# Four modulation vectors of a diffusion layer: three summed by the vector engine during the value and latent projections, one left on the tensor engine

## The chip, the cores and the metric

The kernel runs on one core of a Trainium2 chip. The metric is the device time of one execution in microseconds (us), lower is better; for each kernel the median of several runs is compared.

## What is computed

The reference is one layer of a diffusion backbone over 512 latent tokens with 256 context tokens, model width 1024, all in float32. What matters here is where the modulation vectors come from and where they are used:

```python
sh1, sc1, g1, sh2, sc2, g2 = adaln(c, w_mod, b_mod)        # silu(c) @ w_mod + b_mod, split in six rows of 1024
hx = modulate(rmsnorm(x, norm_attn_g), sh1, sc1)           # h * (1 + scale) + shift
proj = hx @ w_in                                           # queries, latents, keys, values
o_mla = mla_latent_attention(...)                          # latent attention, 8 heads
o_na = neighbourhood_attention(...)                        # 8 x 16 window, 8 heads
mixed = concat(o_mla, o_na) @ w_out
x = x + g1 * mixed
hx2 = modulate(rmsnorm(x, norm_ffn_g), sh2, sc2)
x = x + g2 * hierarchical_moe(hx2, ...)                    # 16 experts, 2 chosen per token
return rmsnorm(x, final_norm_g)
```

`sh1` and `sc1` are needed at once. The four later rows, `g1`, `sh2`, `sc2` and `g2`, are a product of one vector of 1024 numbers with a matrix of 1024 x 4096 (16.8 MB, called `w_mod_b` in the kernel). `g1` is first used when the output projection begins, `sh2` and `sc2` before the experts, `g2` in the experts.

## The kernel before, in words

A float32 product is made of three matmuls (`mm3`, L56 to L59): each operand is split into a rounded high part (ScalarE, a cast) and the rest, the low part (VectorE, a subtraction), and the products high x high, high x low and low x high are summed. `load_split` (L183) loads a weight into one of three buffers `raw` by SyncE's queue and splits it into `wh` and `wl`, two buffers each. ScalarE (ACT), VectorE (DVE), TensorE (PE), GpSimd (POOL) and SyncE (SP, which issues DMAs) run in order, each through its own list; a scheduler of the framework orders these lists from the order of the code and what depends on what.

The stages, with the time at which they run in the profile: normalisation, first modulations and values (`v_part`, to 66 us; the normalised and transposed rows `xnt` are last read by `mod_h`, L274); the key-value latents (L351 to L363: 3 weight batches, 6 row tiles in PSUM banks 0 to 5, to 85 us); the query latents (L364 to L375: 4 weight batches, to 102 us); norms, transposes and the first projections of neighbourhood attention (to 124 us); neighbourhood attention proper (L720 to L793, 32 blocks: 4 pairs p of heads, 2 heads u, 4 query tiles i, to 241 us); latent attention; output projection and routing; 16 experts (from 427 us).

The four later modulations are computed by `mod_rest` (L510), called for every second of the 32 blocks (L746). Each of its 16 calls loads two tiles of `w_mod_b` (128 x 1024, 512 KB each) into `raw` and issues four matmuls of 512 columns on TensorE, with the vector `silu(c)` as a stationary operand of 32 columns (`sstat`, column 0 is the vector, most are zero), at four column positions of the array, so that the four give four parts of the row. 8 calls make the sums of two vectors; after the last of them the bias is added (L525) and the result stored in DRAM as `mod_d` (L526), from where the later stages load it.

The change and the prediction's steps touch `mod_rest`, the pools around `xnt` (L190 to L192), the latents' loops (L351 to L375), what follows them on VectorE (L385 to L416) and the block loop. TensorE's matmuls in float32 appear twice in the trace for each instruction.

Of the kernel before, what the change touches and what calls it, by code (L numbers as in the profile page):

```python
# [8 lines left out]
F32 = mybir.dt.float32  # L9
# [4 lines left out]
OP = mybir.AluOpType  # L14
# [3 lines left out]
P = 128  # L18
D = 1024
KT = 8  # L20
# [18 lines left out]
def hybrid_kernel(tc, nc, x_k, x_q, ctx, cvec, w_mod_a, w_mod_b, b_mod_c, b_mod_r, g_ffn_row,  # L39
                  w_v, w_kv, w_ql, w_qk, g_q, g_kv, w_uq, w_ukv, rel, w_out_a, w_out_b, w_r, b_r,  # L40
                  w_gate, w_up, w_down, g_fin_row, cpk0, cpk, out):
    sy, ac, ve, pe, gp = nc.sync, nc.scalar, nc.vector, nc.tensor, nc.gpsimd

    def pool(name, bufs=1, side="left", space=None):
        kw = dict(name=name, bufs=bufs, reuse_waits="tile")
        if space is None:
            return tc.alloc_tile_pool(side=side, **kw)
        return tc.alloc_tile_pool(space=space, **kw)
# [30 lines left out]
    def copy(dst, src, of=2):  # L79
        turn[0] += 1  # L80
        if turn[0] % of == 1:
            ve.tensor_copy(dst, src)
        else:
            ac.copy(dst, src)
# [60 lines left out]
    gp.dma_start(wr, w_r)  # L145
    gp.dma_start(brb, b_r.to_broadcast([P, 20]))


    chp = pool("chp")
    omp = pool("omp")  # L150
# [13 lines left out]
    sstat = navp.tile([P, KT, 32], F32, name="sstat")  # L164
# [5 lines left out]
    HW = CX + TC  # L170
# [7 lines left out]
    def load(src, n=1024):  # L178
        r = raw_tile()
        sy.dma_start(r[:, :n], src)  # L180
        return r

    def load_split(src, n=1024, r=None):  # L183
        r = load(src, n) if r is None else r
        h = chp.tile([P, 1024], F32R, name="wh", tag="wh", bufs=2)
        l = chp.tile([P, 1024], F32R, name="wl", tag="wl", bufs=2)
        split(h[:, :n], l[:, :n], r[:, :n])
        return h, l

    pa = pool("pa", side="right")  # L190
    xnt = pa.tile([P, KT, HW], F32, name="xnt")
    px = pool("px", side="right")  # L192
    xts = []

# [7 lines left out]
    def bank(*nums):  # L202

        n = taken[nums] = taken.get(nums, -1) + 1
        return psA.tile([P, 512], F32, name="ps", tag=f"b{nums[n % len(nums)]}", bufs=1)
# [105 lines left out]
    def v_part(k, ts):  # L311
        wv_h, wv_l = wv[k // 2]
        s = slice(k % 2 * 512, k % 2 * 512 + 512)
        for t in ts:
            mm3(av[t], hh[:, k, key_cols(t)], hl[:, k, key_cols(t)], wv_h[:, s], wv_l[:, s],
                start=(k == 0), stop=(k == KT - 1))
# [22 lines left out]
    for q in range(2, 4):  # L339
        for k in (2 * q, 2 * q + 1):  # L340
            mod_h(k, 0)
            mod_h(k, 1)
            v_part(k, range(6))
    for t in range(6):
        copy(nav[:, t, :], av[t])


    px.release()
    pl = pool("pl", side="right")
    KB = (0, 3, 6, 8)  # L350
    akv = [bank(i) for i in range(6)]  # L351
    for b in range(3):
        n = KB[b + 1] - KB[b]
        wh, wl = load_split(w_kv[:, KB[b] * 288:KB[b + 1] * 288], n * 288)
        for i in range(n):
            k = KB[b] + i
            s = slice(i * 288, (i + 1) * 288)
            for t in range(6):
                mm3(akv[t][:, 0:288], hh[:, k, key_cols(t)], hl[:, k, key_cols(t)], wh[:, s], wl[:, s],
                    start=(k == 0), stop=(k == KT - 1))  # L360
# [3 lines left out]
    aq = [bank(i) for i in range(4)]  # L364
    for b in range(4):
        wh, wl = load_split(w_ql[b], 768)
        for i in range(2):
            k = 2 * b + i
            s = slice(i * 384, (i + 1) * 384)
            for t in range(4):  # L370
                mm3(aq[t][:, 0:384], hh[:, k, q_cols(t)], hl[:, k, q_cols(t)], wh[:, s], wl[:, s],
                    start=(k == 0), stop=(k == KT - 1))
    qlt = pl.tile([P, 4, 384], F32, name="qlt")
    for t in range(4):
        copy(qlt[:, t, :], aq[t][:, 0:384])  # L375

    krk = pl.tile([P, 6, 32], F32, name="krk")

# [16 lines left out]
    for c in range(2):  # L395
        for b0, n in ((0, 4), (4, 2)):
            tr = bank4(4, 5, 6)
            for i in range(n):
# [5 lines left out]
                                    op0=OP.mult, op1=OP.subtract)  # L404
# [18 lines left out]
    sy.dma_start(qn_dram, qst)  # L423

    pl.release()
    pa.release()


# [36 lines left out]
    nw = pool("nw", side="right")  # L465
# [37 lines left out]
    ve.memset(zero, 0.0)  # L503


    mod_d = tc.dram_tile([2, 4, 512], F32, name="mod_d")
    modf = mod_d.rearrange("r a b -> r (a b)")
    mod_ps = []

    def mod_rest(n):  # L510
        r, k = divmod(n, KT)
        if k == 0:
            br = nw.tile([P, 512], F32, name="br", tag="br", bufs=1)
            ve.memset(br, 0.0)
            rows = br.rearrange("(a b) n -> a b n", b=32)[:, 0, :]
            sy.dma_start(rows, b_mod_r[r])
            mod_ps[:] = bank(7), br, rows
        ps, br, rows = mod_ps
        ws = [load(w_mod_b[r, k, :, q * 1024:(q + 1) * 1024]) for q in range(2)]
        for g in range(4):  # L520
            pe.matmul(ps[g * 32:(g + 1) * 32, :], sstat[:, k, :],
                      ws[g // 2][:, g % 2 * 512:g % 2 * 512 + 512], start=(k == 0), stop=(k == KT - 1),
                      tile_position=(0, g * 32))
        if k == KT - 1:
            ve.tensor_tensor(br, br, ps, op=OP.add)  # L525
            sy.dma_start(mod_d[r], rows)  # L526

    na_heads, na_w, na_ps = {}, {}, {}

# [190 lines left out]
    for b, (p, u, i) in enumerate(blocks):  # L720
        w = b % 8
# [21 lines left out]
        if w == 0 and p:  # L743
            norm_ = normalise_steps(na_ssum[p - 1], nw, onh[:, p - 1, :], onl[:, p - 1, :])
            next(norm_)
        if i % 2:  # L746
            mod_rest(p * 4 + u * 2 + i // 2)
        pull(NS[p][w] - (NS[p][w] > 1))
        if w == 0 and p:
            norm_.send((na_values(p - 1), bank4(4, 5)))  # L750
# [139 lines left out]
    mw = pool("mw")  # L890
# [1028 lines left out]
```

## Time and profile before

| | |
|---|---|
| median of 3 runs | 736.14 us (732.59 to 736.38) |
| the profiled execution | 733.54 us, of which the profile's span is 731.8 us |
| TensorE busy | 698.1 us (95%) |
| VectorE busy | 546.4 us (75%) |
| ScalarE busy | 447.7 us (61%) |
| DMA | 174.6 MB, mean 239 GB/s |

The page of the profile gives the busy time of each engine over the span. A busy share is an average over stages with different limits, so for a change that moves work from one stage to another the stretches are read one by one: how busy each engine is there, and what each engine waited for. "PEld" is the load of stationary operands, which overlaps the matmuls.

### The profile page before, as it was taken

The page shows a single profiled execution, that of the slowest core. Times are in us where ns is not written, and L with a number is a line of the kernel's source. Part 1 is how long each engine was busy: PE and PEld are TensorE (multiplying, and loading weights), DVE is VectorE, ACT ScalarE, POOL GpSimd, SP SyncE. Part 2 cuts the span into 40 slices and gives each one's busy share as a digit, 9 for nine tenths or more (in the row PEclk, how much of TensorE's full clock was granted, in tenths as well). Part 3 has the DMA queues.
Part 4 walks back from the last instruction along what each step waited for, and adds up shares of the span by engine and source line. Part 5 has one row for each costly group of instructions (what it writes and reads, how often), then busy time and mean ns, then how long its engine had stood idle before and what let it go on. Part 6 is the DMA issues. An engine that isn't in the chain of part 4 may idle for free. (4 is left out here: it accounts for less than half of the span.)

```text
span 731.8 us, 10466 instructions
## 1 busy us (share of the span) xinstructions
PE 698.1 (95%) x3918; PEld 516.9 (71%) x3919; DVE 546.4 (75%) x749; ACT 447.7 (61%) x698; POOL 83.7 (11%) x56
## 2 busy tenths in 40 slices
PE   4999999999999999999999679999999999999995
PEld 3678997767765887868658557777777777777773
DVE  4572457766676795656536778999999999999996
ACT  6451355654555455646644377777777777777763
POOL 1010000000000000000010122222222222221310
PEclk9999999999999999999999769999999999999998
DMA  8931238555476821121179979999999999999673
GB/s 319 409 124 60 73 95 279 194 172 190 144 236 202 288 88 43 60 76 54 59 252 364 346 244 364 362 372 370 353 360 357 358 352 350 358 354 379 239 132 116
DMA packets 39336, 174.58 MB, mean 239 GB/s; under 512 B 5711, under 2 KB 7191, under 8 KB 26992
## 3 DMA queue, kind: packets, MB, share of 16 engines
q1 hardware_dynamic: 34880, 163.72, 61.4%
q0 software_dynamic: 4112, 10.06, 6.3%
q8 instruction: 32, 0.52, 0.3%
q14 instruction: 24, 0.20, 0.1%
q10 hardware_dynamic: 288, 0.08, 0.0%
HBM read 163.00 MB, written 14.79 MB: 243 GB/s over the span
## 5 line engine op out<-in xcount | busy, mean ns | idle before, releaser
L1376 DVE TENSOR_TENSOR el<-ew,eh 128x2048 fp32r<-128x2048 f32 (+1 forms) x106 | 220.6, 2087 | 17.3 <-ACT eh L1373 13.7
L1373 ACT CAST eh<-ew 128x1024 fp32r<-128x1024 f32 x190 | 190.1, 1050 | 43.9 <-PE s L59 29.4
L57 PE MATMUL s<-eh,xh 128*96 128x512 f32 x260 | 104.7, 403 | 1.1 <-ACT xh L62 1.1
L59 PE MATMUL s<-eh,xl 128*96 128x512 f32 x260 | 103.3, 397 | 0.0
L58 PE MATMUL s<-el,xh 128*96 128x512 f32 x260 | 102.8, 395 | 0.0
L1588 POOL DMA_INDIRECT ya_d<-yo,idx x14 | 45.5, 3251 | 140.7 <-DVE yo L1592 140.7
L59 PEld LDWEIGHTS s<-eh,xl 128*96 128x96 f32 x260 | 42.3, 163 | 19.3 <-DVE xl L63 0.7
L57 PEld LDWEIGHTS s<-eh,xh 128*96 128x96 f32 x260 | 42.4, 163 | 18.3 <-ACT xh L62 1.4
L58 PEld LDWEIGHTS s<-el,xh 128*96 128x96 f32 x260 | 42.5, 164 | 17.5 <-DVE el L1376 0.2
L57 PE MATMUL y<-eh,ghh 128*96 128x512 f32 x120 | 48.2, 401 | 0.0
L59 PE MATMUL y<-eh,ghl 128*96 128x512 f32 x120 | 47.3, 394 | 0.0
L58 PE MATMUL y<-el,ghh 128*96 128x512 f32 x120 | 47.2, 393 | 0.0
L470 DVE TENSOR_REDUCE nm<-s 128x1 f32<-128x768 f32 x32 | 30.5, 954 | 19.1 <-PE s L59 18.9
L57 PE MATMUL ps<-wh,hh 128*128 128x512 f32 (+2 forms) x128 | 43.9, 345 | 0.5 <-ACT hh L275 0.3
L59 PE MATMUL ps<-wh,hl 128*128 128x512 f32 (+2 forms) x128 | 43.5, 345 | 0.2 <-DVE hl L277 0.2
L58 PE MATMUL ps<-wl,hh 128*128 128x512 f32 (+2 forms) x128 | 43.4, 341 | 0.0
L1303 POOL MEMSET xg<- 128x1024 f32 x2 | 1.9, 954 | 322.1 <-DMA g<-mod_d 322.1
L57 PE MATMUL ps<-hh,wh 128*128 128x512 f32 (+1 forms) x96 | 36.4, 379 | 0.0
L946 ACT ACTIVATE pr<-s,nm 128x768 f32<-128x768 f32 x32 | 29.1, 908 | 9.8 <-DVE nm L470 9.6
L59 PE MATMUL ps<-hh,wl 128*128 128x512 f32 (+1 forms) x96 | 34.4, 359 | 0.0
L58 PE MATMUL ps<-hl,wh 128*128 128x512 f32 (+1 forms) x96 | 34.2, 357 | 0.0
L1261 POOL DMA_INDIRECT xg<-hx_d,idx x16 | 24.2, 1510 | 65.9 <-PE t L1519 46.7
(360 smaller groups left out, 1455.8 us busy)
## 6 DMA issues: line engine op xcount, KB each, us to landing
ew<-w_gate SPq DMA_DIRECT2D x32, 1024.0 KB, 8.6
ew<-w_up SPq DMA_DIRECT2D x32, 1024.0 KB, 8.0
ew<-w_down SPq DMA_DIRECT2D x32, 1024.0 KB, 9.4
raw<-w_mod_b SPq DMA_DIRECT2D x32, 512.0 KB, 3.8
wm<-w_mod_a SPq DMA_DIRECT2D x16, 512.0 KB, 10.8
raw<-w_qk SPq DMA_DIRECT2D x8, 512.0 KB, 3.4
raw<-w_v SPq DMA_DIRECT2D x4, 512.0 KB, 10.5
ya_d<-zero SPq DMA_DIRECT2D x8, 256.0 KB, 3.2
```

Of the source, the lines that this page charges most:

```text
L57: pe.matmul(ps, lh, rh, start=start, stop=False)
L58: pe.matmul(ps, lh, rl, start=False, stop=False)
L59: pe.matmul(ps, ll, rh, start=False, stop=stop)
L470: ve.tensor_reduce(out=nm, in_=s, axis=AX.X, op=OP.max, negate=True)
L946: ac.activation(pr, s, AF.Exp, bias=nm, accum_out=mla_ssum[h // 2][:, t, h % 2:h % 2 + 1])
L1261: ins = gp.indirect_dma_start(out=xg[e % NX][slice(0, CAP), :], out_offset=None, in_=hx_d, in_offset=bass.IndirectOffsetOnAxis(ap=idx[slic ...
L1303: gp.memset(x_, 0.0)
L1373: ac.copy(wh[:, cs], r[:, cs])
L1376: ve.tensor_tensor(wl[:, cs], r[:, cs], f(wh[:, cs]), op=OP.subtract)
L1588: gp.indirect_dma_start(out=ya_d, out_offset=bass.IndirectOffsetOnAxis(ap=idx[rows, 1, e:e + 1], axis=0), in_=yo[rows, :], in_offset=None, ...
```

## The change

Three of the four later vectors (`g1`, `sh2`, `sc2`) are now summed on VectorE: tile by tile of `w_mod_b`, `macc = w * silu(c) + macc`, with one value of `silu(c)` per partition. 24 such steps (three sums of 8 tiles) are spread over the code of the values and latents by the table `MA`: 8 before the values are copied out, 5, 5 and 1 with the three key-value batches, 3 and 2 with the first query batches. Five buffers `mw` hold the tiles; they are loaded from GpSimd's queue, each next load being issued behind the step that frees its buffer. The sum over the partitions is then made by eight matmuls with a column block of ones (`mod_out`): four of 512 columns, four of 256. The fourth vector, `g2`, stays in `mod_rest`, which now makes 8 calls (one for each head of each pair) with one tile and four matmuls of 256 columns. `xnt` has a pool of its own, so that it is given up, with the pool `px`, before the latents.

```diff
+    MA = (8, 5, 5, 1, 3, 2, 0, 0)
...
-    xnt = pa.tile([P, KT, HW], F32, name="xnt")
+    pxn = pool("pxn", side="right")
+    xnt = pxn.tile([P, KT, HW], F32, name="xnt")
...
+    px.release()
+    pxn.release()
+    mod_d = tc.dram_tile([2, 4, 512], F32, name="mod_d")
+    modf = mod_d.rearrange("r a b -> r (a b)")
+    pm_ = pool("pm", side="right")
+    mws = []
+    MW = 5
+    def mod_load():
+        if len(mws) < 24:
+            n, k = divmod(len(mws), KT)
+            mws.append(pm_.tile([P, 1024], F32, name="mw", tag="mw", bufs=MW))
+            gp.dma_start(mws[-1], w_mod_b[n // 2, k, :, n % 2 * 1024:n % 2 * 1024 + 1024])
+    for _ in range(MW):
+        mod_load()
+    ones = pm_.tile([P, 32], F32, name="ones")
+    ve.memset(ones, 1.0)
...
+        ve.memset(mbs[n], 0.0)
...
+        sy.dma_start(r, at(b_mod_r))
+    def mod_add(m):
+        for _ in range(m):
+            n, k = divmod(done[0], KT)
+            w = mws[done[0]]
+            if k == 0:
+                ve.tensor_scalar(macc[n], w, sstat[:, k, 0:1], None, op0=OP.mult)
+            else:
+                ve.scalar_tensor_tensor(macc[n], w, sstat[:, k, 0:1], macc[n], op0=OP.mult, op1=OP.add)
+            done[0] += 1
+            mod_load()
+    def mod_out(r):
+        ps = bank(7)
+        w_ = (512, 256)[r]
+        for g in range(4):
+            a = macc[g // 2][:, g % 2 * 512:g % 2 * 512 + 512] if r == 0 else macc[2][:, g * 256:g * 256 + 256]
+            pe.matmul(ps[g * 32:(g + 1) * 32, 0:w_], ones, a, start=True, stop=True, tile_position=(0, g * 32))
+        ve.tensor_tensor(mbs[r][:, 0:w_], mbs[r][:, 0:w_], ps[:, 0:w_], op=OP.add)
+        sy.dma_start(mod_at[r](mod_d), mrow[r])
+    done = [0]
+    mod_add(MA[0])
     for t in range(6):
         copy(nav[:, t, :], av[t])
-    px.release()
...
         wh, wl = load_split(w_kv[:, KB[b] * 288:KB[b + 1] * 288], n * 288)
+        mod_add(MA[1 + b])
...
         wh, wl = load_split(w_ql[b], 768)
+        mod_add(MA[4 + b])
...
         copy(qlt[:, t, :], aq[t][:, 0:384])
+    for r in range(2):
+        mod_out(r)
...
     pl.release()
+    pm_.release()
     pa.release()
...
-    def mod_rest(n):
-        r, k = divmod(n, KT)
+    def mod_rest(k):
...
-        ws = [load(w_mod_b[r, k, :, q * 1024:(q + 1) * 1024]) for q in range(2)]
+        w = load(w_mod_b[1, k, :, 1024:2048])
         for g in range(4):
-            pe.matmul(ps[g * 32:(g + 1) * 32, :], sstat[:, k, :],
-                      ws[g // 2][:, g % 2 * 512:g % 2 * 512 + 512], start=(k == 0), stop=(k == KT - 1),
-                      tile_position=(0, g * 32))
+            pe.matmul(ps[g * 32:(g + 1) * 32, 0:256], sstat[:, k, :], w[:, g * 256:g * 256 + 256],
+                      start=(k == 0), stop=(k == KT - 1), tile_position=(0, g * 32))
...
-        if i % 2:
-            mod_rest(p * 4 + u * 2 + i // 2)
+        if i == 3:
+            mod_rest(p * 2 + u)
```

The scheduler puts the new steps between the older work of VectorE. Its list from the split of the first query batch to that of the second and the norm of the latents, before (`wl` is the low part of a weight, `kvt` the key-value latents copied out of PSUM, `kr` and `krk` the rotary key):

```order
L63 TENSOR_TENSOR wl_878<-raw_875,wh_877 128x768
L82 COPY kvt_864<-ps_696 128x288
L82 COPY kvt_864<-ps_698 128x288
L82 COPY kvt_864<-ps_700 128x288
L390 TENSOR_TENSOR kr1_1003<-kvt_864,cka_112 128x128
L391 TENSOR_TENSOR kr2_1004<-kvt_864,cka_112 128x4x16
L392 TENSOR_TENSOR kr2_1004<-kvt_864,cka_112 128x4x16
L393 TENSOR_TENSOR krk_1000<-kr1_1003,kr2_1004 128x128
L394 COPY krk_1000<-kvt_864 128x64
L63 TENSOR_TENSOR wl_908<-raw_905,wh_907 128x768
L94 TENSOR_SCALAR nwv_1017<-sm_67 128x6
```

and the same place after the change (`mw` is a tile of `w_mod_b`, `macc1` and `macc2` the second and third sum):

```order
L63 TENSOR_TENSOR wl_966<-raw_963,wh_965 128x768
L386 SCALAR_TENSOR_TENSOR macc1_714<-mw_770,sstat_104,macc1_714 128x1024
L384 TENSOR_SCALAR macc2_715<-mw_773,sstat_104 128x1024
L82 COPY kvt_952<-ps_751 128x288
L82 COPY kvt_952<-ps_753 128x288
L386 SCALAR_TENSOR_TENSOR macc2_715<-mw_776,sstat_104,macc2_715 128x1024
L82 COPY kvt_952<-ps_755 128x288
L386 SCALAR_TENSOR_TENSOR macc2_715<-mw_839,sstat_104,macc2_715 128x1024
L63 TENSOR_TENSOR wl_999<-raw_996,wh_998 128x768
L386 SCALAR_TENSOR_TENSOR macc2_715<-mw_842,sstat_104,macc2_715 128x1024
L63 TENSOR_TENSOR wl_1031<-raw_1028,wh_1030 128x768
L386 SCALAR_TENSOR_TENSOR macc2_715<-mw_845,sstat_104,macc2_715 128x1024
```

Of the 24 steps 15 now stand before the split of the first query batch, 19 before that of the second, 20 and 23 before those of the third and fourth; the rotary key and the scaling of `kvt` (L387, now L447), which stood before the split of the third query batch, stand behind nearly all or all of the 24.

On TensorE, the place where the query latents end, after the change (`ps<-macc` are the sums over partitions, `ps<-c_58,kvt` the transposes of the latents; before, ten of these transposes came directly):

```order
L395 MATMUL ps<-macc_713,ones 32x512 x2
L395 MATMUL ps<-macc_714,ones 32x512 x2
L459 MATMUL ps<-c_58,kvt 128x128 x8
L395 MATMUL ps<-macc_715,ones 32x256 x4
L459 MATMUL ps<-c_58,kvt 128x128 x2
L57 MATMUL ps<-hh,wh 128x512
```

TensorE's list there now holds eight new matmuls, the last four behind the last step of VectorE.

In the last quarter of neighbourhood attention, before, the four matmuls of one call stand apart in twos (`L606`, `L607` are scores, `L634` transposes, L57 to L59 values of latent attention):

```order
L59 MATMUL ps<-wh,kvo 128x512
L521 MATMUL ps<-raw,sstat 32x512 x2
L606 MATMUL ps<-kk,qh 128x512
L607 MATMUL ps<-kk,ql_1128 128x512
L634 MATMUL ps<-c_58,pr 128x128 x2
L521 MATMUL ps<-raw,sstat 32x512 x2
L634 MATMUL ps<-c_58,pr 128x128 x2
```

and after the change the last call stands as one piece of four:

```order
L665 MATMUL ps<-kk,ql_1233 128x512
L692 MATMUL ps<-c_58,pr 128x128 x4
L580 MATMUL ps<-raw,sstat 32x256 x4
L57 MATMUL ps<-wh,kvh 128x512
```

Before, the list holds 13 pieces of four and 6 of two; after, 7 pieces of four, and the first call split into one and three.

## Rows read from the trace of the kernel before

**Rows 1.** The page, part 1: the span, and TensorE's busy time.

```profile
span 731.8 us, 10466 instructions
PE 698.1 (95%) x3918; PEld 516.9 (71%) x3919; DVE 546.4 (75%) x749; ACT 447.7 (61%) x698; POOL 83.7 (11%) x56
```

**Rows 2.** Busy time by stretch: stretch, length, five engines' busy us, clock, DMA share, GB/s.

```profile
20.00:40.00 20.00, 19.34 (x205) 13.69 (x196) 10.62 (x25) 8.97 (x15) 0.00 (x0) 1.00 1.03 405
57.00:66.30 9.30, 9.30 (x43) 7.70 (x42) 2.96 (x4) 2.10 (x3) 0.00 (x0) 1.00 0.14 42
66.30:85.20 18.90, 18.90 (x145) 18.90 (x144) 3.96 (x7) 4.17 (x10) 0.00 (x0) 1.00 0.20 64
85.20:102.00 16.80, 16.80 (x100) 16.76 (x99) 8.77 (x23) 7.11 (x19) 0.00 (x0) 1.00 0.33 107
102.00:112.00 10.00, 10.00 (x58) 7.95 (x57) 7.51 (x19) 8.84 (x21) 0.00 (x0) 1.00 0.35 123
124.00:206.00 82.00, 82.00 (x525) 58.26 (x523) 54.69 (x102) 43.20 (x92) 0.00 (x0) 1.00 0.56 186
206.00:238.00 32.00, 31.46 (x176) 17.71 (x173) 21.70 (x39) 19.50 (x40) 0.00 (x0) 1.00 0.63 211
```

**Rows 3.** Groups by line on TensorE, 100 to 245 us: busy, mean ns | idle before.

```profile
L521 PE MATMUL ps<-raw,sstat 128*32 128x512 f32 x128 | 20.3, 605 | 0.5 <-DMA raw<-w_mod_b 0.5
```

**Rows 4.** TensorE's timeline around two pieces: start us, us, what.

```profile
122.91 0.39 PE L607 MATMUL ps<-kk,ql 128*128 128x512 f32 x1
...
124.07 0.40 PE L59 MATMUL ps<-hh,wl 128*128 128x512 f32 x1
124.40 1.06 PE L521 MATMUL ps<-raw,sstat 128*32 128x512 f32 x8
125.40 0.50 PE L57 MATMUL ps<-hh,wh 128*128 128x512 f32 x1
125.74 0.40 PE L58 MATMUL ps<-hl,wh 128*128 128x512 f32 x1
125.98 0.40 PE L59 MATMUL ps<-hh,wl 128*128 128x512 f32 x1
...
225.29 1.05 PE L521 MATMUL ps<-raw,sstat 128*32 128x512 f32 x4
```

**Rows 5.** TensorE's timeline: narrower matmuls of the same kind, 128 columns.

```profile
43.48 1.30 PE L246 MATMUL ps<-wm,sstat 128*32 128x128 f32 x40
45.37 0.65 PE L246 MATMUL ps<-wm,sstat 128*32 128x128 f32 x16
```

**Rows 6.** Groups by line and shape on VectorE, to 130 us: busy us, mean ns.

```profile
L276 DVE SCALAR_TENSOR_TENSOR xnt<-xnt,ab,hh 128x576 f32<-128x576 f32 x8 | 6.4, 813 | 1.9 <-ACT hh L275 1.9
L276 DVE SCALAR_TENSOR_TENSOR xnt<-xnt,ab,hh 128x256 f32<-128x256 f32 x8 | 3.8, 480 | 0.7 <-ACT hh L275 0.7
L220 DVE TENSOR_SCALAR xa<-xa,sm 128x1024 f32<-128x1024 f32 x2 | 1.5, 754 | 0.1
L514 DVE MEMSET br<- 128x512 f32 x1 | 0.5, 485 | 0.1
```

**Rows 7.** TensorE's timeline: the first matmuls of the first and second query batch.

```profile
85.31 0.33 PE L57 MATMUL ps<-wh,hh 128*128 128x384 f32 x1
...
89.49 0.33 PE L57 MATMUL ps<-wh,hh 128*128 128x384 f32 x1
```

**Rows 8.** DMA issues: queue, count, KB each, median us from issue to landing.

```profile
raw<-w_mod_b SPq DMA_DIRECT2D x32, 512.0 KB, 3.8
...
x<-ya_d POOLq DMA_DIRECT2D x4, 512.0 KB, 8.4
```

**Rows 9.** GpSimd's own issues of direct DMAs, late and early in the kernel.

```profile
L1640 POOL DMA_DIRECT2D x<-ya_d x4: 965/1428/1921, 699.4 to 701.1; - x4
...
DMA to landing us min/median/max: 5.6/8.4/11.3
...
1.32 0.70 POOL L141 DMA_DIRECT2D mp<-b_mod_c  x1 [0.85 <-POOLq L1909]
```

More of the change, by code (lines that the diff above doesn't have):

```diff
@@ L343, in hybrid_kernel @@
             v_part(k, range(6))
+    px.release()
[14 more added lines that the diff above has]
+    ve.memset(ones, 1.0)
+    mbs, macc = [], []
+    for n in range(2):
+        mbs.append(pm_.tile([P, 512], F32, name=f"mb{n}"))
+        ve.memset(mbs[n], 0.0)
+    for n in range(3):
+        macc.append(pm_.tile([P, 1024], F32, name=f"macc{n}"))
+    mrow = [b_.rearrange("(a b) n -> a b n", b=32)[:, 0, 0:w_] for b_, w_ in zip(mbs, (512, 256))]
+    mod_at = [lambda d: d[0], lambda d: d[1, 0:2].rearrange("a (b n) -> (a b) n", n=256)]
+    for r, at in zip(mrow, mod_at):
+        sy.dma_start(r, at(b_mod_r))
[19 more added lines that the diff above has]
+    mod_add(MA[0])
     for t in range(6):
         copy(nav[:, t, :], av[t])
-    px.release()
     pl = pool("pl", side="right")
@@ L503, in hybrid_kernel @@
     ve.memset(zero, 0.0)
-    mod_d = tc.dram_tile([2, 4, 512], F32, name="mod_d")
-    modf = mod_d.rearrange("r a b -> r (a b)")
     mod_ps = []
-    def mod_rest(n):
-        r, k = divmod(n, KT)
+    def mod_rest(k):
+        last = mod_d[1, 2:4].rearrange("a (b n) -> (a b) n", n=256)
         if k == 0:
-            br = nw.tile([P, 512], F32, name="br", tag="br", bufs=1)
+            br = nw.tile([P, 256], F32, name="br", tag="br", bufs=1)
             ve.memset(br, 0.0)
             rows = br.rearrange("(a b) n -> a b n", b=32)[:, 0, :]
-            sy.dma_start(rows, b_mod_r[r])
+            sy.dma_start(rows, b_mod_r[1, 2:4].rearrange("a (b n) -> (a b) n", n=256))
             mod_ps[:] = bank(7), br, rows
         ps, br, rows = mod_ps
-        ws = [load(w_mod_b[r, k, :, q * 1024:(q + 1) * 1024]) for q in range(2)]
+        w = load(w_mod_b[1, k, :, 1024:2048])
         for g in range(4):
-            pe.matmul(ps[g * 32:(g + 1) * 32, :], sstat[:, k, :],
-                      ws[g // 2][:, g % 2 * 512:g % 2 * 512 + 512], start=(k == 0), stop=(k == KT - 1),
-                      tile_position=(0, g * 32))
+            pe.matmul(ps[g * 32:(g + 1) * 32, 0:256], sstat[:, k, :], w[:, g * 256:g * 256 + 256],
+                      start=(k == 0), stop=(k == KT - 1), tile_position=(0, g * 32))
         if k == KT - 1:
-            ve.tensor_tensor(br, br, ps, op=OP.add)
-            sy.dma_start(mod_d[r], rows)
+            ve.tensor_tensor(br, br, ps[:, 0:256], op=OP.add)
+            sy.dma_start(last, rows)
     na_heads, na_w, na_ps = {}, {}, {}
```

## The prediction

> **What bounds the kernel now.** I read the page first, then the busy time by stretch, then the timeline of TensorE where the change takes work away and the groups of VectorE where it adds some. The page has TensorE busy for 698.1 of 731.8 us [rows 1]; no other engine comes near. The stretches show whether that holds where the change is made. In neighbourhood attention TensorE is busy for 82.00 of 82.00 us from 124 to 206 us and for 31.46 of 32.00 us after that, at a granted clock of 1.00, while VectorE has 54.69 and 21.70 us, ScalarE 43.20 and 19.50 us [rows 2]. Full-width matmuls follow each other there every 0.24 us (125.74 to 125.98) without a gap [rows 4]. The stage lasts as long as TensorE's list. In the stretches of the latents, 57 to 102 us, TensorE is busy throughout as well, but VectorE only for 2.96 of 9.30, 3.96 of 18.90 and 8.77 of 16.80 us, and the DMAs move 42, 64 and 107 GB/s [rows 2], where the same engines moved 405 GB/s between 20 and 40 us. The change takes work from the first place and puts it into idle time of the second.
>
> **What is removed from TensorE.** The 128 records of L521 are 64 matmuls, busy for 20.3 us in all [rows 3]. In TensorE's list they form 19 pieces: 13 of four matmuls (8 records) and 6 of two (4 records). A piece costs more than its width: from the matmul before it (124.07) to the second one behind it (125.74) 1.67 us pass where two ordinary steps take 0.48 [rows 4], so 1.2 us. A piece of two is as long as one of four, 1.05 against 1.06 us [rows 4], since the four run side by side. 19 x 1.2 = 22.8 us. The one wait for a tile, 0.5 us [rows 3], goes with them.
>
> **What is added to TensorE.** In the 8 remaining calls the matmuls are 256 columns wide, in 9 pieces. No row has that width; 128 columns are the nearest. From 16 to 40 records the time grows from 0.65 to 1.30 us [rows 5], 0.22 us for eight. Eight of 512 columns would then be 0.87 us and a rest of 0.2, which makes the 1.06 us of rows 4; eight of 256 columns are 0.43 + 0.2, about 0.65 us. A piece then costs 1.2 - 0.4 = 0.8 us (bounds 0.6, by 128 columns, and 1.2, by 512). 9 x 0.8 = 7.2 us. The sums over partitions are one piece of 512 columns and one of 256: 1.2 + 0.8 = 2.0 us. Together TensorE's list becomes 22.8 - 7.2 - 2.0 = 13.6 us shorter, with the wait 14.1 us.
>
> **What is added to VectorE.** A step reads two float32 operands of 1024 columns and a value per partition. The same instruction takes 0.813 us at 576 and 0.480 us at 256 columns [rows 6], 1.04 ns a column, so 1.28 us at 1024; the three that begin a sum are plain scalings, 0.754 us [rows 6]. 21 x 1.28 + 3 x 0.75 = 29.1 us. Two memsets at 0.485 us [rows 6] (the third has 32 columns), and two additions of a bias, priced at the 0.813 and 0.480 us of rows 6, bring 2.3 us: 31.4 us. From 57 to 112 us VectorE is idle for 6.34 + 14.94 + 8.03 + 2.49 = 31.8 us [rows 2]. The new work just fills it. That is the tight place: the engine runs in order, and between the steps stand the splits and copies for which TensorE waits.
>
> **Who waits there.** The first query batch starts at 85.31 us and the second at 89.49 [rows 7], so batches come every 4.18 us and the fourth starts at about 97.85. Its split stands behind 23 steps. Step by step, with older work at its old prices, VectorE reaches the first query batch's split at about 82 us, in time, but ends the first copy of `kvt`, behind 17 steps, at 85.6, about 0.3 us late for the bank that the first query tile needs; the second split is done at 90, 0.2 us late; the fourth just in time. The scaling of the key-value latents, which was done before the third batch's split, now ends at about 102: TensorE stands at the sums over partitions then, so most of it is covered, but VectorE comes into the norms and rests of 102 to 112 us with some 2 us of backlog. I charge 1 us for that. Semaphore waits between dependent steps and the DMA below make the rest of a charge of 4 us; the bounds are 0 and 8 us (a quarter of the idle time not being usable).
>
> **The loads.** 24 x 0.524 MB = 12.6 MB come on top of 3.4 MB that these stretches move already (42 x 9.3, 64 x 18.9 and 107 x 16.8, in GB/s and us [rows 2]). At 405 GB/s [rows 2] that takes 39.5 of the 45 us: it fits, with little to spare. For VectorE to be in time for the fourth split, 23 steps must end by 96.8 us, from 57 us on one in 1.8 us. With five buffers the time of one is a fifth of its round: landing, plus the step of 1.28 us. Landing takes 3.8 us on SyncE's queue for tiles of this size [rows 8], a round of 5.1 us or 1.0 us a step; 8.4 us in the median on GpSimd's [rows 8], 1.9 us; 11.3 us at most, behind an issue that itself takes up to 1.9 us [rows 9], 2.9 us. The 8.4 us are from loads that also add to what they load into, so plain loads should be nearer to 3.8; I take 1.7 us, at the limit. Before, the issues were SyncE's; its queue loses 24 of 32, and the two small loads of the bias are put ahead of the query weights, which wait for their buffers anyway.
>
> **What else moves.** GpSimd's four memsets of `ql` now stand behind its 24 issues, which end by 97 us, and behind the reads of the older tiles at that place, to about 112 us. At some 0.5 us each (the 128x512 memset of VectorE [rows 6]) they end by 115 us; the first matmul that needs them starts at 122.91 [rows 4]. With less filling between scores and transposes, chains of VectorE and ScalarE in the last quarter of the stage may show: 1 us (bounds 0 and 3). All later stages wait for neighbourhood attention and move forward as a whole.
>
> **The sum.** 733.5 - 14.1 + 4 + 1 = 724.4 us on the profiled execution's own scale. The four times known (732.6, 733.5, 736.1, 736.4) have a mean of 734.7, 1.1 us above it, so I predict **725.5 us** for the median.
>
> **The rivals.**
> 1. *The tiles come too slowly.* GpSimd's queue is slower than SyncE's, VectorE stands at a step and the splits behind it wait, and TensorE with them. For it: 8.4 against 3.8 us [rows 8]. Against it: those loads add. Each 0.1 us a step beyond 1.8 costs 2.2 us; at 2.35 us the gain of 14.1 - 2 is gone. At the 2.9 us above, 22 x 1.1 = 24 us are lost: 733.5 - 12.1 + 24 = 745 us. Slower, 11%. A GpSimd issue took 0.97 to 1.92 us beside a busy VectorE, 0.70 us beside an idle one [rows 9], so VectorE does hold such issues up, though not by much. The Trainium skill (SBUF — State Buffer, sections "SBUF: two separate sides" and "A bandwidth-pool intuition that's wrong") says that descriptors of GpSimd's DMAs cannot be written while VectorE runs a copy or scaling in a mode that takes both port pairs, and names 620 ns becoming about 3100 ns. By that figure as the time of a step, an estimate from the page, 22 x 1.3 = 29 us would be lost and the time would be 750 us; but its section "Who interferes with whom" counts plain copies and `tensor_scalar` to this mode and not `tensor_tensor`, and 21 of the 24 steps here are of two tensors. I give it 3 of the 11%.
> 2. *The freed time is not taken.* The matmuls taken out filled TensorE's waits for softmax, and waits take their place; or VectorE's in-order list costs its upper bound. Half of the gain returned as waits: 733.5 - 14.1 + 7 + 4 = 730.4, 731.5 as a median, no change that can be told. Against it: VectorE is busy for 67% and ScalarE for 53% of 124 to 206 us [rows 2], and nothing but 0.5 us of waits stands in the way of TensorE. 13%. The Trainium skill (Perfetto Trace Analysis, section "Identifying the Most-Contended Engine") says that matmul busy time does not tell how close TensorE is to its limit; the even steps of 0.24 us say that here it does.
> 3. *The new steps do not run where they are meant*, because the buffers come free late. Then they run from 85 us on, and this becomes rival 1.
>
> **How the numbers follow.** The forecast has 76%. Its own bounds go from 14.1 us of gain (719.4) to 14.1 - 8 - 3 = 3.1 us. The range takes in most of rival 2 and none of rival 1: 719 to 732 us. A measurement can tell about 0.5%, 3.7 us, from no change. Faster by more than that 76%, within it 13%, slower 11%.
>
> **What would show it.** Right: L580 with 64 records of about half the time; neighbourhood attention from first scores to end some 13 us shorter, still without waits of TensorE; VectorE at nine tenths or more from 57 to 102 us; DMA at 350 GB/s or more there; the fourth query batch starting within 3 us of its old time. Wrong: TensorE waiting on `wl` or `kvt` behind steps that wait for `mw` (rival 1), landing times of `mw` above 9 us, or new waits of TensorE for ScalarE or VectorE from 124 us on (rival 2).

## The result and the profile after

The changed kernel takes **726.55 us** (median of 4 runs, 725.2 to 729.04), the kernel before 735.4 us beside it: a ratio of 0.9891 with a 95% interval of 0.9861 to 0.9921. A second comparison (experiment 5) gave 0.9904 (0.9874 to 0.9933). Both intervals lie below 1: the change gains about 1%. The forecast was 725.5 us, faster, with a range of 719 to 732 us. The profiled execution took 727.33 us, its span is 725.5 us.

The page after, part 1, answers to [rows 1]:

```profile
span 725.5 us, 10436 instructions
PE 685.6 (94%) x3870; PEld 515.3 (71%) x3871; DVE 571.5 (79%) x776; ACT 447.5 (62%) x698; POOL 95.5 (13%) x80
```

TensorE has 12.5 us less work, VectorE 25.1 us more. Busy time by stretch after the change (the columns of [rows 2]):

```profile
57.00:66.30 9.30, 9.30 (x43) 7.70 (x42) 5.19 (x6) 2.10 (x3) 2.74 (x6) 1.00 0.88 309
66.30:85.20 18.90, 18.17 (x136) 17.73 (x135) 15.28 (x16) 3.04 (x5) 5.68 (x11) 1.00 0.95 350
85.20:102.00 16.80, 14.31 (x85) 14.03 (x85) 16.55 (x24) 6.93 (x20) 3.78 (x8) 1.00 0.88 320
102.00:112.00 10.00, 10.00 (x67) 7.66 (x66) 8.51 (x21) 7.64 (x18) 0.81 (x2) 1.00 0.40 133
```

VectorE's new work is in these stretches, and TensorE, which was busy throughout, now stands for 0.73 and 2.49 us. Its waits from 50 to 250 us after the change (total us, times, longest us; `nav` are the values copied out of PSUM, `pt` the transposed exponentials of the softmax, `pr` those before the transposes), and the start of the second query tile on its timeline:

```profile
PE ps L57 <- DVE kvt L82: 2.5, 1, 2.5
PE s L57 <- DVE q L906: 0.9, 1, 0.9
PE ps L701 <- DVE pt L82: 0.8, 1, 0.8
PE ps L57 <- DVE nav L82: 0.7, 1, 0.7
```

```profile
89.31 0.44 PE L57 MATMUL ps<-wh,hh 128*128 128x384 f32 x1 [2.49 <-DVE kvt L82]
```

The wait for `q` lies in latent attention and was there before. The other three are new. VectorE's timeline just before the longest of them shows why:

```profile
77.56 1.28 DVE L386 SCALAR_TENSOR_TENSOR macc<-mw,sstat,macc 128x1024 f32<-128x1024 f32 x1 [1.20 <-DMA mw<-w_mod_b]
79.07 1.28 DVE L386 SCALAR_TENSOR_TENSOR macc<-mw,sstat,macc 128x1024 f32<-128x1024 f32 x1 [0.23 <-DMA mw<-w_mod_b]
81.39 1.28 DVE L386 SCALAR_TENSOR_TENSOR macc<-mw,sstat,macc 128x1024 f32<-128x1024 f32 x1 [1.03 <-DMA mw<-w_mod_b]
83.23 1.28 DVE L386 SCALAR_TENSOR_TENSOR macc<-mw,sstat,macc 128x1024 f32<-128x1024 f32 x1 [0.56 <-DMA mw<-w_mod_b]
84.87 1.29 DVE L386 SCALAR_TENSOR_TENSOR macc<-mw,sstat,macc 128x1024 f32<-128x1024 f32 x1 [0.35 <-DMA mw<-w_mod_b]
86.07 0.95 DVE L63 TENSOR_TENSOR wl<-raw,wh 128x768 fp32r<-128x768 f32 x1
...
88.80 0.81 DVE L82 COPY kvt<-ps 128x288 f32<-128x288 f32 x2
```

Five steps in a row wait 3.37 us for tiles. The split of the first query batch, meant for 82 us, starts at 86.07, and the copies of `kvt`, which TensorE needs for its next bank, at 88.80.

Where the time went is best read from milestones on TensorE: the first and last start of the scores and of the last transposes behind neighbourhood attention, before and after:

```profile
L606 PE MATMUL ps<-kk,qh x32: 392/396/499, 122.6 to 229.1; 128*128 128x512 f32 x32
L486 PE MATMUL ps<-c,rsb x16: 272/273/331, 152.2 to 241.5; 128*128 128x128 f32 x16
```

```profile
L664 PE MATMUL ps<-kk,qh x32: 389/394/504, 127.8 to 223.3; 128*128 128x512 f32 x32
L547 PE MATMUL ps<-c,rsb x16: 272/273/329, 155.5 to 232.8; 128*128 128x128 f32 x16
```

The last matmul of the query latents, before and after:

```profile
101.80 0.34 PE L59 MATMUL ps<-wh,hl 128*128 128x384 f32 x1
105.71 0.34 PE L59 MATMUL ps<-wh,hl 128*128 128x384 f32 x1
```

3.9 us are lost there. The latents begin at nearly the same time in both executions (the first matmul of the key-value latents starts at 66.26 and 66.18 us), so from their own start to this matmul they take 35.5 us before and 39.5 after. To the first scores 5.2 us are lost. From there to the last transposes 118.9 us became 105.0: 13.9 us won. At this point the kernel is 8.7 us ahead, close to the difference of the medians (8.85 us). The profiled executions themselves end only 6.3 us apart, and experiments 5 and 6 take that up.

### The profile page after: what moved, and what is told of

Read it like the earlier page. It is cut to its first block, busy times and chain, and to the rows that moved or that the text cites. A ratio compares the mean times of both kernels' runs of the same rounds, so it can differ in the third digit from the quotient of the medians.

```text
span 725.5 us, 10436 instructions
## 1 busy us (share of the span) xinstructions
PE 685.6 (94%) x3870; PEld 515.3 (71%) x3871; DVE 571.5 (79%) x776; ACT 447.5 (62%) x698; POOL 95.5 (13%) x80
## 5 line engine op out<-in xcount | busy, mean ns | idle before, releaser
L57 PE MATMUL s<-eh,xh 128*96 128x512 f32 x260 | 104.5, 402 | 0.9 <-ACT xh L62 0.9
L59 PE MATMUL s<-eh,xl 128*96 128x512 f32 x260 | 103.1, 396 | 0.0
L59 PEld LDWEIGHTS s<-eh,xl 128*96 128x96 f32 x260 | 42.2, 162 | 19.1 <-DVE xl L63 0.6
L57 PEld LDWEIGHTS s<-eh,xh 128*96 128x96 f32 x260 | 42.3, 163 | 18.0 <-ACT xh L62 1.2
L57 PE MATMUL y<-eh,ghh 128*96 128x512 f32 x120 | 48.1, 401 | 0.0
L57 PE MATMUL ps<-wh,hh 128*128 128x512 f32 (+2 forms) x128 | 44.2, 348 | 3.7 <-DVE kvt L82 2.5
L59 PE MATMUL y<-eh,ghl 128*96 128x512 f32 x120 | 47.3, 395 | 0.0
L59 PE MATMUL ps<-wh,hl 128*128 128x512 f32 (+2 forms) x128 | 43.5, 345 | 0.3 <-DVE hl L279 0.3
L57 PE MATMUL ps<-hh,wh 128*128 128x512 f32 (+1 forms) x96 | 36.1, 376 | 0.0
L59 PE MATMUL ps<-hh,wl 128*128 128x512 f32 (+1 forms) x96 | 34.4, 358 | 0.0
```

Source lines behind the costliest of these rows:

```text
L57: pe.matmul(ps, lh, rh, start=start, stop=False)
L59: pe.matmul(ps, ll, rh, start=False, stop=stop)
```

## The experiments

My theory: TensorE's shorter list in neighbourhood attention gives the gain, VectorE's new work in the latents takes some 4 us back. Rivals: the tiles' loads set the pace; freed time turns into waits; the loss comes from elsewhere. A ratio is always to the kernel before on the same chip. The diffs are shortened, `...` marks what is left out.

**1. No steps on VectorE.**

```diff
-    for _ in range(MW):
-        mod_load()
...
-        for _ in range(m):
+        for _ in range(0):
...
+        gp.memset(macc[n], 0.0)
```

> The 24 steps on the vector engine and the loads of their tiles are left out (the three sums stay zero, so g1, sh2 and sc2 hold the bias alone); everything on TensorE stays as after the change. My theory (the charge of 4 us comes from VectorE's new work): the start of the latents' transposes goes back from 105.98 to within 0.5 us of the old 101.98 us, the waits for kvt at 89.3 us (2.49 us) and for nav (0.73 us) are gone, and the median is 735.4 - 14.1 + 1 = 722.3 us (ratio 0.982). Rival (the 4 us come from elsewhere, such as the changed order or the DMAs at the pools' release): the transposes stay near 106 us and the time near 726.5 us (0.988). In both, neighbourhood attention from first scores to end lasts as long as after the change, 104.6 us.

Measured: 724.58 us, ratio 0.9857 (0.9834 to 0.988). The waits for `kvt` and `nav` are gone, the last matmul of the query latents starts at 102.04 us, and neighbourhood attention takes 105.0 us (124.2 to 229.2). So the 3.9 us of the latents are VectorE's steps and their loads, as the theory has it. At the end only some 2 us of them are left by the medians, and the intervals of the two ratios overlap; where the rest goes is in experiment 5.

**2. Seven and three tiles.**

```diff
-    MW = 5
+    MW = 7
```

(and 3 in the other kernel.)

> Seven buffers for the tiles of w_mod_b in place of five, the order of VectorE's list unchanged. If the tile waits (5.7 us of VectorE after the change) come from the length of a round, seven buffers take most of them away, the split of the first query batch moves from 86.1 to about 83.5 us and the kvt copies with it, and TensorE's wait at 89.3 us falls from 2.49 us below 0.5 us: 724 us (ratio 0.985). If the DMA engines are the limit, more loads in flight only land later (near 9.5 us instead of 6.9), the tile waits stay above 4 us and the time at 726.5 us (0.988).

> Three buffers for the tiles of w_mod_b in place of five. After the change a tile landed 6.9 us after its issue and a step took 1.28 us, a round of 8.2 us. If a round stays so long, three buffers give a step every 2.7 us, 0.9 us beyond the 1.8 us that the fourth query batch needs: 22 x 0.9 = 20 us are lost, and the time is about 746 us (ratio 1.015), the case of my rival 1. If the landing is long only because five loads share the DMA engines, three in flight land in about 4.5 us, a step every 1.9 us, and 2 to 4 us are lost: 729 to 731 us (0.992 to 0.994). VectorE then stands at the steps for mw, and TensorE waits for wl behind it.

Measured: seven 725.93 us, ratio 0.9876 (0.9851 to 0.9901); three **742.39 us**, ratio 1.0105 (1.0072 to 1.0137), slower than before. Issues and time to landing of the tiles with three, five (the changed kernel) and seven buffers:

```profile
mw<-w_mod_b POOLq DMA_DIRECT2D x24, 512.0 KB, 5.2
```

```profile
mw<-w_mod_b POOLq DMA_DIRECT2D x24, 512.0 KB, 6.9
```

```profile
mw<-w_mod_b POOLq DMA_DIRECT2D x24, 512.0 KB, 8.4
```

Fewer loads in flight land sooner, but not in proportion. A round is landing, issue (0.53 us) and step (1.28 us): 7.0, 8.7 and 10.2 us, by the number of buffers 2.3, 1.7 and 1.5 us a step. From the first step to the last the timelines have one in 2.4, 1.9 and 1.8 us, so only with three does the round alone set the pace. The wait for `kvt` is 2.5 us with five (1.3 to 2.5 us in the five executions here that leave the latents and five buffers as they are), gone with seven, and 6.8 us with three:

```profile
PE ps L57 <- DVE kvt L82: 6.8, 2, 4.3
PE ps L459 <- DVE kvt L447: 2.3, 2, 2.0
PE ps L57 <- DVE nav L82: 2.2, 2, 1.9
PE ps L395 <- DVE mb L396: 1.3, 1, 1.3
```

So both are at work: the number of buffers in a round, and a landing that grows with the number in flight. With five buffers the loads decide in part; with three, rival 1 of the prediction comes true. Its price was too low: the 24 steps lie 2.4 us apart (59.8 to 114.9 us), which by the prediction's 2.2 us for each 0.1 us beyond 1.8 makes 736 us. The steps end behind the query latents (their last matmul starts at 112.87 us), so that all that follows waits as well, and the first scores start 14.1 us later than after the change. Seven take TensorE's long wait away, but the latents end only 1.1 us earlier (104.62 us). This execution came to them late: their first matmul starts at 67.50 us and not at 66.18, and the delay is there at TensorE's first matmul of a split weight already (21.91 against 20.59 us), before the first new load. From their own start the latents take 37.1 us, against 35.5 before and 38.5 to 39.5 with five tiles (four executions). So about half of the 4.0 us lost there come from the wait for tiles; the rest stays, with VectorE busy for 16.16 of 16.80 us from 85.2 us on. The two times, 725.93 and 726.55 us, cannot be told apart.

**3. Loads on SyncE's queue.**

```diff
-            gp.dma_start(mws[-1], w_mod_b[...])
+            sy.dma_start(mws[-1], w_mod_b[...])
```

> The tiles of w_mod_b are loaded from SyncE's queue, as they were before, instead of GpSimd's. SyncE issues in order, and 19 of the 24 loads, each waiting for a buffer that a step frees, stand ahead of all four loads of the query weights. My theory (the queue matters by what stands behind a waiting load, not by its speed): the tiles land in 4 to 6 us, but the query weights are issued only when the 19th step has ended, at about 91 us in place of some 75, their splits come 5 to 8 us late and TensorE waits for wh and wl there: 732 to 736 us (ratio 0.996 to 1.001), the gain nearly gone. Rival (the queue is of no importance as long as the DMA engines have room): within 1 us of 726.5 us.

Measured: **740.27 us**, ratio 1.0069 (1.0039 to 1.0099). SyncE's issues:

```profile
60.30 32.37 SPq L361 DMA_DIRECT2D mw<-w_mod_b  x19
92.72 1.45 SPq L181 DMA_DIRECT2D raw<-w_ql  x3
```

The tiles land in 5.6 us, faster than on GpSimd's queue, and still the kernel is slower: the query weights leave at 92.72 us. From 85.2 to 102 us TensorE is busy for 8.07 of 16.80 us, at a granted clock of 0.73. The mechanism is the expected one; I had put the loss against the changed kernel at 5.5 to 9.5 us, it was 13.7. The fallen clock and the changed order (transposes of the latents wait 7.9 us for VectorE) are part of that, in shares not taken apart.

**4. What a piece costs.** The kernel before without any piece, and the changed kernel without those of `g2`:

```diff
-        ws = [load(w_mod_b[r, k, :, q * 1024:(q + 1) * 1024]) for q in range(2)]
-        for g in range(4):
-            pe.matmul(...)
         if k == KT - 1:
-            ve.tensor_tensor(br, br, ps, op=OP.add)
```

> The kernel before without the weight loads, the matmuls and the additions of mod_rest (all four later vectors hold the bias alone), to price the 19 pieces by themselves. The prediction took 1.2 us a piece: 22.8 us and 0.5 us of waits less, and the stretch from first scores to the last transposes behind neighbourhood attention falls from 118.9 to about 95.6 us. Rival (a piece costs less than the timeline made it, or waits take the place of some): the changed kernel without g2 still took 99.7 us there, without any piece; then 19 pieces cost 19.2 us, 1.0 us each, the stretch is 99 to 100 us, and TensorE shows new waits for ScalarE or VectorE of 1 us or more.

> The eight calls of mod_rest lose their loads, matmuls and the addition (g2 holds the bias alone); the rest is as after the change. My theory (TensorE's list sets the length of neighbourhood attention, and a piece of four matmuls of 256 columns costs 0.8 us more than no piece): nine pieces, 7.2 us less, from 726.55 to 719.4 us (ratio 0.978), and first scores to end of neighbourhood attention falls from 104.6 to about 97.5 us. Rival (freed time not taken, softmax chains on VectorE and ScalarE show): less than half of it, above 723 us, with new waits of TensorE for VectorE or ScalarE from 130 us on.

Measured: 716.05 us, ratio 0.9756 (0.9738 to 0.9774), and 723.39 us, ratio 0.9864 (0.9828 to 0.99). First and last scores and transposes of the first, then of the second:

```profile
L600 PE MATMUL ps<-kk,qh x32: 388/396/505, 122.1 to 212.6; 128*128 128x512 f32 x32
L486 PE MATMUL ps<-c,rsb x16: 272/273/331, 145.1 to 221.9; 128*128 128x128 f32 x16
```

```profile
L659 PE MATMUL ps<-kk,qh x32: 391/396/505, 127.5 to 217.8; 128*128 128x512 f32 x32
L547 PE MATMUL ps<-c,rsb x16: 270/272/331, 150.4 to 227.2; 128*128 128x128 f32 x16
```

Without pieces the stage takes 99.8 and 99.7 us, the same in both kernels. So the 19 pieces of before cost 118.9 - 99.8 = 19.1 us, 1.0 each and not 1.2, and the 9 narrow ones 105.0 - 99.7 = 5.3 us, 0.6 each and not 0.8. The timelines agree: from the start of a piece to the start of what follows it, the 19 pieces take 19.0 us in all and the 9 narrow ones 5.1 us. The 0.2 us that the prediction added for the steps beside a piece do not show in the stage. The rival's 99 to 100 us were right, though its new waits are small (0.6 us for `pr`, 0.3 for `pt`). The second kernel's four times spread from 720.75 (the profiled execution) to 727.01 us, so its median says less than its stage.

**5. Both kernels once more, unaltered**, for the 2.4 us that the profiled executions lose behind the routing.

> The kernel before unaltered, for the same place. If the gather's delay comes with the change, the gap from the first slot sums to the first expert matmul is 7 to 8 us again. If it varies, it may be 10 to 11 us, and the time then stands 2 to 3 us above the first profiled execution's 733.5 us.

> The changed kernel unaltered, for its first expert gather: in the profile of after it was issued at 415.2 us, 4.5 us after its indices, and TensorE waited 3.46 us for it, while in the one profile of before it was issued 1.4 us after them, without such a wait; the kernels with seven and three tiles and without g2 waited 3 to 4 us there as well. If the delay comes with the change, it recurs here: from the first slot sums to the first expert matmul 10 to 11 us. If it varies from execution to execution, it is as likely to be gone (7.2 us). The median is 726.5 us in either case (ratio 0.988).

Measured: before 734.41 us, ratio to itself 0.9988 (0.9965 to 1.001); after 729.4 us. VectorE's indices and GpSimd's first gather in the second execution of before, then in the first of after:

```profile
419.19 0.17 DVE L1206 TENSOR_SCALAR idx<-x 96x16 int32<-96x16 f32 x1 [1.13 <-PE x L1202]
```

```profile
423.60 1.08 POOL L1261 DMA_INDIRECT xg<-hx_d,idx  x1 [5.15 <-DVE va L1183]
```

```profile
410.68 0.17 DVE L1264 TENSOR_SCALAR idx<-x 96x16 int32<-96x16 f32 x1 [1.13 <-PE x L1260]
```

```profile
415.19 1.08 POOL L1319 DMA_INDIRECT xg<-hx_d,idx  x1 [5.24 <-DVE va L1241]
```

The gather comes 4.4 and 4.5 us behind its indices in both kernels. In the first execution of before it was 1.4 us (419.42 to 420.82). The delay varies from execution to execution and is not the change's. From the indices to the end of the span it is 312.4 us in that first execution, 314.6 in the second, 314.8 and 314.0 us in the two of after: the first profile of before is the odd one. Its early gather is not the reason. In the second execution of after and in the kernels of experiments 1 and 7 the gather starts 1.0 us behind its indices, and the rest takes 314.0, 315.0 and 313.9 us; in the eight executions where it starts 3.5 to 5.5 us behind them, the rest takes 313.8 to 314.9 us. Why the first profile of before has 312.4 us stays open.

The second execution of after (span 731.0 us) shows three more losses that vary. It comes to the latents 1.6 us later (their first matmul starts at 67.81 us). In them TensorE stood for 2.2 us, and the granted clock fell behind it; columns as above:

```profile
88.00:90.00 2.00, 0.03 (x1) 0.00 (x0) 2.00 (x3) 1.03 (x2) 0.52 (x1) 1.00 0.91 322
90.00:92.00 2.00, 1.73 (x8) 1.73 (x9) 2.00 (x4) 1.66 (x7) 0.55 (x2) 0.83 0.95 353
92.00:94.00 2.00, 2.00 (x8) 2.00 (x7) 2.00 (x3) 1.71 (x7) 0.90 (x2) 0.50 0.90 280
94.00:96.00 2.00, 2.00 (x11) 2.00 (x11) 1.40 (x2) 0.00 (x0) 1.14 (x3) 0.82 0.99 393
```

At 0.50 (1.2 GHz) these matmuls start every 0.32 us, at 1.00 every 0.17. The last matmul of the query latents starts at 108.26 us, 2.55 us later than in the first execution, which had stood for 2.49 us and kept its clock: 1.6 us of that are the late start, 0.9 us were lost in the latents themselves (40.5 against 39.5 us). In the routing VectorE waits for the store of an older tile of rows (`hx_d`) before it may write `t`, and TensorE loses 3.7 us behind it:

```profile
404.79 0.69 DVE L1296 TENSOR_TENSOR t<-x,gs 128x512 f32<-128x512 f32 x1 [4.33 <-DMA hx_d<-t]
```

The same wait (3.9 us) is what took the time back in the profiled execution of experiment 1. Unlike the gather's delay, it moves all that follows: from the last transposes behind neighbourhood attention to the indices, 181.6 and 181.4 us pass in these two executions, and 177.8 to 178.2 us in the nine where the wait is at most 0.8 us.

**6. The stores on GpSimd's queue**, away from the experts' weights:

```diff
-        return sy.dma_start(hx_d[t * P:(t + 1) * P, :], h2s[t]).ins.name
+        return gp.dma_start(hx_d[t * P:(t + 1) * P, :], h2s[t]).ins.name
```

> As after the change, but the four stores of the experts' rows (hx_d) go out on GpSimd's queue instead of SyncE's, where they stand among the loads of the experts' weights (DMA share above 0.9 there). In every profile but the first of before, the routing loses 3 to 4 us in one of two ways: the first gather comes 3 us late behind the last store, or VectorE waits 4 us for an earlier store before it may write t again. If the queue is the cause, both are gone (gather 1.0 to 1.4 us after its indices, no wait of t for hx_d above 1 us) and the time is about 726.5 - 3 = 723.5 us (ratio 0.984). If the DMA engines themselves are the cause, the stores land as late from another queue and the time stays at 726 to 728 us; if GpSimd's issues come late, it gets longer.

Measured: 727.7 us, ratio 0.9919 (0.9892 to 0.9946): no gain. Yet both delays are gone in the profiled execution: the gather starts 1.9 us after its indices (411.54), the first expert's transposes at 416.1 instead of 419.8 us. The expert begins earlier, but at a fallen clock and with few loads under way:

```profile
416.10:421.10 5.00, 2.75 (x11) 1.62 (x11) 3.65 (x7) 1.00 (x2) 1.18 (x2) 0.50 0.81 253
421.10:426.10 5.00, 5.00 (x13) 2.95 (x13) 1.38 (x2) 2.46 (x3) 0.00 (x0) 0.50 0.44 122
426.10:431.10 5.00, 4.13 (x17) 2.66 (x18) 4.42 (x3) 5.00 (x6) 0.00 (x0) 1.00 1.00 352
```

After the change the first expert began 3.7 us later, at the same clock, and got the higher one back sooner after its start:

```profile
419.80:424.80 5.00, 4.05 (x14) 2.71 (x15) 2.57 (x3) 3.40 (x4) 0.96 (x1) 0.50 0.83 261
424.80:429.80 5.00, 5.00 (x20) 3.42 (x19) 3.46 (x3) 3.18 (x4) 0.00 (x0) 0.82 0.94 316
```

From the indices to the end it takes 315.9 us, the longest of all executions here. So an earlier gather brought nothing, as in experiment 5. That SyncE's queue is the cause of the delays fits this run but is not shown: it is one execution, and the first one of before had neither delay on that queue. What sets the pace of the first expert (the clock, or weights that can only be loaded when it has used the older ones) was not taken apart.

**7. The copies on ScalarE.**

```diff
-        copy(kvt[:, t, :], akv[t][:, 0:288])
+        ac.copy(kvt[:, t, :], akv[t][:, 0:288])
```

(and the same for `nav`.)

> All copies of the values and of the key-value latents out of PSUM on ScalarE, in place of every second one on VectorE. If TensorE's waits of 2.49 us (kvt) and 0.73 us (nav) come from those copies standing behind VectorE's steps, both are gone, ScalarE (7 of 17 us busy there) takes the copies without a new wait, the last matmul of the query latents starts 3 us earlier than after the change (105.7), at about 102.7 us, and the time is 726.5 - 3 = 723.5 us (ratio 0.984). If VectorE's backlog as a whole is what counts, the wait only moves to the split of the second query batch: above 105 us, and 726 us. If the routing stage waits for its DMAs whatever comes earlier, the 3 us are seen at 103 us but not at the end.

Measured: 727.62 us, ratio 0.9885 (0.9847 to 0.9923). The two waits are gone, but 1.6 us of new ones for the splits `wl` and 0.9 for `kvo` appear; the query latents' last matmul starts at 103.80 us and the end does not move. From their own start the latents take 38.0 us: the place of the copies in VectorE's list is worth at most 1.5 of the 4.0 us lost there. The rest stays, with the new waits for VectorE's splits, so its backlog counts for more.

**8. The fourth vector on VectorE too, and then with seven tiles.**

```diff
-        for g in range(4):
-            pe.matmul(ps[g * 32:(g + 1) * 32, 0:256], sstat[:, k, :], w[:, g * 256:g * 256 + 256], ...)
+        ve.scalar_tensor_tensor(br, w, sstat[:, k, 0:1], br, op0=OP.mult, op1=OP.add)
         if k == KT - 1:
+            for g in range(4):
+                pe.matmul(ps[g * 32:(g + 1) * 32, 0:256], ones4, br[:, g * 256:g * 256 + 256], ...)
```

> The fourth vector as well summed on VectorE, during neighbourhood attention: eight steps of 1.28 us (10.2 us in all) in place of nine pieces of TensorE; one sum over partitions of 256 columns stays (0.8 us), the bias is put into the sum, and the zeros that clear a buffer in DRAM are half as wide. TensorE's list becomes 7.2 - 0.8 = 6.4 us shorter; leaving the pieces out altogether brought 5.3 us in that stage. If VectorE (busy for 73% of 130 to 206 us) has room between its chains, 4 to 5 us are won: 722 us (ratio 0.982). If its steps get into the chains of softmax, new waits of TensorE for nm, pr or pt show from 128 us on and the gain is 0 to 2 us, 725 to 727 us, or turns into a loss.

> Two edits together: all four vectors summed on VectorE (the fourth during neighbourhood attention) and seven buffers for the tiles of the first three. By the profiles of the two alone, the latents end about 1 us earlier than after the change (104.6 against 105.7) and neighbourhood attention is some 1 to 3 us shorter than 105.0 us. If the two add up: 3 us below the changed kernel's 727.8 us (median of its nine times), about 724.5 us (ratio 0.985). If they are covered by the routing and the first expert, which begin at a fallen clock, 726 to 727 us (0.988 to 0.990).

Measured: 725.04 us, ratio 0.9858 (0.9816 to 0.99), and **721.57 us** (720.55 to 723.4), ratio **0.9832** (0.9817 to 0.9847). The second is the fastest of the study that computes the whole layer: its interval lies below that of the changed kernel. Its milestones:

```profile
L667 PE MATMUL ps<-kk,qh x32: 387/394/500, 127.3 to 219.0; 128*128 128x512 f32 x32
L547 PE MATMUL ps<-c,rsb x16: 270/273/330, 155.9 to 229.4; 128*128 128x128 f32 x16
```

Neighbourhood attention takes 102.1 us instead of 105.0 (103.9 us with five tiles, where the granted clock is 0.92 from 210 us on). The latents end 0.8 us earlier, although they begin 1.3 us later: 3.4 us at 229.4. Of the 5.3 us that leaving the pieces out brings, the one piece left, the steps and new waits (1.0 us for `pr`, 0.7 for `kk`, the keys) take 2.4 back.

## Why the prediction was right, by its steps

The forecast for the median was 1.1 us off (725.5 us, measured 726.55). At the end of neighbourhood attention, where all that is new lies behind, the profiles stand 8.7 us apart and the sum had 9.1. Both halves of the mechanism hold: 13.9 us won in neighbourhood attention (15.1 by the sum, with its tail of 1 us), 5.2 us lost before it (6.0 by the sum, the charge of 4 and the sums over partitions of 2.0). That the net is so near is in part luck: terms erred by up to 3.7 us and made up for each other. Of the signs named for being right several were not met as stated: from 57 to 102 us VectorE is busy for 82% and the DMAs move 330 GB/s, not nine tenths and 350; the fourth query batch starts 3.9 us late and not within 3. And the sign of rival 1, TensorE waiting for `kvt` behind steps that wait for `mw`, did appear; its 2.49 us lay within the charge.

- **Removed from TensorE, 22.8 us: too much, 19.1 measured.** The step that failed is the price of 1.2 us a piece, which added to a piece what its neighbours took longer in one place of the timeline [rows 4]; the mean over all 19 is 1.0 (experiment 4), what a piece takes from its own start to that of the next group.
- **Added to TensorE.** A narrow piece was priced at 0.8 us, measured 0.6, for the same reason. Eight records of this width do last 0.64 us in the sums over partitions, as worked out by interpolation (0.65). One record takes 391 ns against 605 [rows 3], two thirds and not the half that I had announced:

```profile
L580 PE MATMUL ps<-raw,sstat 128*32 128x256 f32 x64 | 5.7, 391 | 0.0
```

- **Added to VectorE.** A step takes 1.280 us, as extrapolated from narrower rows of the same instruction [rows 6]:

```profile
L386 DVE SCALAR_TENSOR_TENSOR macc<-mw,sstat,macc 128x1024 f32<-128x1024 f32 x21 | 26.9, 1280 | 5.8 <-DMA mw<-w_mod_b 5.7
```

- **The charge of 4 us: near in size, wrong in place.** It held 1 us for the backlog behind the latents, so 3 us for the latents themselves, where 3.9 were lost; the sums over partitions and the backlog behind them cost 1.3 us (5.2 - 3.9) where I had 2.0 + 1. I had VectorE's list late by 0.3 us at the first query batch and the rest in small waits. It was one wait of 2.49 us, and its cause is mainly the 5.7 us for which VectorE stood at tiles: with seven tiles it is gone. Nine tenths of VectorE's time were reached only from 85 us on (98%); before, it stood at 56% and 81%.
- **The loads: the round right, the pace not.** 1.7 us a step was taken, at the limit of 1.8. The round measured gives 1.7, and the landing (6.9 us in the median, 9.9 at most) lies between the two bounds of 3.8 and 8.4 us. But the steps came one in 1.9 us, with VectorE's older work between them and a wait of 2.2 us for the first key-value weight (`wh`, from ScalarE), and the 23rd ended at 99.4 us and not by 96.8.
- **Rival 1** was two buffers or one queue away, as experiments 2 and 3 show. The prediction read from [rows 9] that a busy VectorE holds GpSimd's issues up; that does not show here. Beside a VectorE busy for up to 98% the issues took 527 to 820 ns, 530 in the median. The Trainium skill's rule that descriptors of GpSimd's DMAs cannot be written until VectorE releases the shared port (SBUF — State Buffer, section "A bandwidth-pool intuition that's wrong") does not show here either. The same page of the Trainium skill, in its section "Who interferes with whom", says that `tensor_tensor` has no mode that takes both port pairs. It does not name the instruction of the steps, but 21 of the 24 read two tensors as well, so the trace agrees with it.
- **Rival 2** did not come. From 124 to 245 us TensorE has one new wait of 0.8 us (`pt`), as the tail of 1 us had it.
- **Rival 3** did not come: the first step starts at 56.38 us.
- **Later stages move as a whole:** true up to the indices of the experts (8.7 us in the first profiles). Behind them the first profile of before was 1 to 3 us shorter than all others, and in some executions a wait for a store adds up to 3.7 us ahead of them (experiment 5).

## What to carry to other kernels

Work moved from a full engine into another's idle time costs what it delays in that engine's list. By the sum the idle time just sufficed here (31.4 of 31.8 us), but the steps wait for loads, and each wait is passed on to the copies and splits behind them. So look at the round of a buffer (landing, issue, step), divide it by the number of buffers and compare it with the time that a step may take: three buffers made a loss, seven saved a wait. Price a piece of work by leaving all of them out once, since the price from one place of a timeline, with the neighbours' share, was 20% too dear. Measure a stage from its own start: an execution may come to it 1 to 2 us early or late.

## What was not expected of the hardware

- The landing time of a 512 KB load grew with the number in flight: 5.2, 6.9 and 8.4 us for three, five and seven on GpSimd's queue, 5.6 us for five on SyncE's.
- A pause of TensorE of about the same length (2.49 and 2.2 us) cost its clock in one execution and not in the other. Where it did, the latents took 40.5 us from their own start and not 39.5.
- In the routing two delays of up to 5 us vary from execution to execution. The gather's delay behind its indices leaves no trace in the time to the end (313.9 to 315.0 us with 1.0 us of it, 313.8 to 314.9 with 3.5 to 5.5). The wait of `t` for a store does: 3.7 us in the second execution of after.
